# Splitting a weight chunk in four pieces ahead of the last squares, and splitting one chunk ahead in the second pass

## The chip, the core and the metric

The kernel runs on one core of a Trainium2 chip. The metric is the device time of one execution in microseconds. An execution is also profiled: the profile lists each instruction of TensorE (PE, and PEld for its weight loads), VectorE (DVE), ScalarE (ACT), GpSimd (POOL) and SyncE (SP, whose queue here issues most DMAs), with its start, its duration and what it waited for.

## The reference

One layer of a decoder trunk over 16 meta tokens and 256 tokens, of 2048 channels. What matters here is its beginning: the norm, and the combined projection whose columns are taken apart.

```python
h = jnp.concatenate([meta_b, x], axis=1)            # 16 + 256 rows of 2048
u = rms_norm(h, g_pre_mix[l])
proj = u @ w_in[l]
z_pool, v_conv, g_conv, gate_a, gate_b = jnp.split(proj, splits, axis=-1)
y_a = causal_multiscale_pool(z_pool, w_pool_grp[l], pool_scale[l]) @ w_pool_out[l]
y_b = conformer_conv(v_conv, g_conv, w_dw[l], b_dw[l],
                     conv_ln_g[l], conv_ln_b[l]) @ w_conv_out[l]
m = jax.nn.sigmoid(gate_a) * y_a + jax.nn.sigmoid(gate_b) * y_b
h = h + rms_norm(m @ w_o[l], g_post_mix[l])
u = rms_norm(h, g_pre_mlp[l])
f = jnp.square(jax.nn.relu(u @ w_up[l])) @ w_down[l]
h = h + rms_norm(f, g_post_mlp[l])
```

In `conformer_conv`, v times sigmoid(g) goes through a causal depthwise convolution of 31 taps. All is float32.

## The kernel before

**Weights come in chunks.** A chunk is 1 MB of float32: 128 partitions by 2048 columns. Its raw form is loaded by SyncE's queue into one of three rooms (`raws`, L252 and L254). It is then split in two numbers, a high part (a copy to fp32r on ScalarE, L259) and a low part (raw minus high on VectorE, L262), and PE multiplies with both: `mm3` (L447) issues three matmuls for each 128 x 128 block, high weights with u's high part, high weights with u's low part, low weights with u's high part. There are three rooms each for raw, high and low. So chunk n is loaded when the low part of chunk n-3 has been made, and its high part is written when PE is done with chunk n-3.

**The first pass** (chunks 0 to 3, `FIRST` = 4) makes the first 256 columns each of v and g for all 272 tokens, four accumulators wide, while x is still coming in. It is a loop over the 16 blocks of 128 channels: product k on PE (`product_of`), transposes of x for the blocks to come (`x_tile`: PE L396, then the scaled high and low parts of u at L397 and L398), and the splits of the weights' rows (`row`), of which each chunk has four here. Into the same loop are put the squares of x and of the meta tokens, halves of a row block at a time (`squares_of`, L406, on ScalarE, in place), whose sums give the norm. The meta tokens' natural layout, `m_in`, is loaded for these squares alone (L355); `x_in` is the layout of x's blocks.

After product 13 chunk 4 is split whole. After the loop `scale_roots` (L420 to L431) takes the roots and makes diagonals of them, `diag`; there a small activation (`warm_up`) brings in the table that holds the sigmoid.

**The second and third pass** are calls of `project`, for v and for g of the next 256 columns; each uses two chunks (4 and 5, then 6 and 7). Ahead of each chunk's matmuls `fetch` splits the chunk and those that follow, up to two ahead, and opens (loads) them where they are not open yet. After each half of the columns `drain` issues what is pending: after the first half of chunk 4 `after_first`, which turns the diagonals into a row of scales (`pb` on PE, L437; copied to `rb` on VectorE, L439) and applies it to the first pass's v (L520); after the second half `tap_columns`, which transposes rows of vectors (L326) and the taps (L589) on PE into PSUM tiles of the same two rooms that pb comes from, and g's part (L527). Later drains issue the convolution, tap by tap (L513 on VectorE).

Every engine works through its own list in the order in which the program issues it: the schedule is written out by hand. PE, ScalarE and VectorE meet only at data and at rooms that have to come free.

The chunks' loads are issued on SyncE's queue in this order: x block 0 and chunk 0 interleaved, x block 1, chunk 1, x block 2, chunk 2 in four loads, x block 3, `m_in`, chunk 3 in four loads, chunk 4, 5, 6 and so on.

Of the kernel before, what the change touches and what calls it, by code (L numbers as in the profile page):

```python
# [10 lines left out]
AF = mybir.ActivationFunctionType  # L11
# [5 lines left out]
CW = 512  # L17
# [83 lines left out]
def hybrid_block(ctx: ExitStack, tc: tile.TileContext, ins: dict, out: bass.AP):  # L101
    nc = tc.nc
    x = ins["x"][0]
    meta = ins["meta"]
    T, D = x.shape
    M = meta.shape[0]
    L = M + T
    NT = T // P
    KD = D // P
    w_in = ins["w_in"][0]  # L110
    w_grp = ins["w_pool_grp"][0]
    NG, GD, _ = w_grp.shape
# [22 lines left out]
    def f32(ap):  # L135
        return ap.bitcast(F32)
# [18 lines left out]
    def flush(n=0):  # L155
        while len(late) > n:
            late.pop(0)()
# [28 lines left out]
    HALF = (2 * CK, CW // 2)  # L186
# [4 lines left out]
    FIRST = len(stream)  # L191
# [35 lines left out]
    def part_tile(tag, n, standing=False):  # L227

        key = f"{tag}{n % 3}"
        room = ready.pop(key) if key in ready else part_room(key, f"{tag}_{n}")  # L230
        place = 2 if standing and tag == "hi" else 1
        shift = (place - 1 - 3 * KEYS.index(key)) % 4 * LINE
        return room[:, shift:shift + CK * CW]

    def open_chunk(loads=None):

        n = at["n"]
        at["n"] += 1
        src, (rows, width) = stream[n]
        raw = raws.tile([P, CK * CW], F32, tag="raw", name=f"raw_{n}")  # L240
        hi, lo = (part_tile(tag, at["parts"], n in standing_chunks) for tag in ("hi", "lo"))
        at["parts"] += 1
        flat, (raw, hi, lo) = raw, (t.rearrange("p (k c) -> p k c", k=rows) for t in (raw, hi, lo))
        if n < FIRST:
            dst = raw.rearrange("p k (h c) -> p k h c", h=2)
            for load in loads or [(slice(i, i + 2), BOTH, nc.sync) for i in range(0, rows, 2)]:
                if callable(load):
                    load()
                    continue
                sl, halves_, queue = load  # L250
                for k in range(sl.start, sl.stop):
                    queue.dma_start(dst[:, k, halves_], src[:, k, halves_])  # L252
        else:
            nc.sync.dma_start(raw, src)  # L254
        pieces = rows if n < FIRST else 1
        k = rows // pieces

        def high(sl, cs):
            nc.scalar.copy(hi[:, sl, cs], raw[:, sl, cs])  # L259

        def low(sl, cs):
            nc.vector.tensor_sub(lo[:, sl, cs], raw[:, sl, cs], f32(hi[:, sl, cs]))  # L262

        def piece(i, cs):
            def f():
                sl = slice(i * k, (i + 1) * k)
                high(sl, cs)
                low(sl, cs)
            return f
        todo = [piece(i, slice(0, width)) for i in range(pieces)]  # L270
        if n == 0:
            todo[:1] = [piece(0, slice(h * HALF_CW, (h + 1) * HALF_CW)) for h in range(2)]
        opened.append((hi, lo, todo, flat))

    def split_pieces(c):
        while opened[c][2]:
            opened[c][2].pop(0)()

    def fetch(ahead=2):

        for c in range(ahead + 1):
            if c == len(opened) and at["n"] < len(stream):
                open_chunk()
            if c < len(opened):
                split_pieces(c)
        flush()
        return opened.pop(0)[:2]
# [10 lines left out]
    def warm_up(func):  # L298

        nc.scalar.activation(warm, ones[:, 0:1], func)  # L300
# [3 lines left out]
    m_in = big.tile([M, D], F32, tag="a", name="m_in")  # L304
# [9 lines left out]
    def load_rows(queue, *names):  # L314
        rows = tmp.tile([48, P], F32, tag="g", name=f"rows_{names[0]}")
        n = 0
        for name in names:
            v = ins[name][0].rearrange("(k p) -> k p", p=P)
            queue.dma_start(rows[n:n + v.shape[0], :], v)
            n += v.shape[0]  # L320
        return rows, n, names[0]
# [10 lines left out]
    def load_x(queue, b, ts=slice(0, NT), cs=(0, 2)):  # L332

        sl = slice(b * CW + cs[0] * CW // 2, b * CW + cs[1] * CW // 2)
        queue.dma_start(x_in[:, ts, sl], xv[:, ts, sl])
# [14 lines left out]
    load_x(nc.sync, 1)  # L350
    open_chunk()
    load_x(nc.sync, 2)
    open_chunk()
    load_x(nc.sync, 3)
    nc.sync.dma_start(m_in, meta)  # L355
    other_rows = load_rows(nc.gpsimd, "pool_scale", "b_dw", "conv_ln_g", "conv_ln_b", "g_pre_mlp")
    taps_in = big.tile([TAPS, CC], F32, tag="c", name="taps_in")
    nc.gpsimd.dma_start(taps_in, w_dw)
# [13 lines left out]
    u = big.tile([P, KD, 2, -(-L // (4 * LINE)) * 4 * LINE], F32R, tag="um", name="u")[:, :, :, :L]  # L372
# [29 lines left out]
    def squares_of(t, b):  # L402

        sl = slice(b * D // 2, (b + 1) * D // 2)
        src, n = (x_in[:, t, sl], P) if t < NT else (m_in[:, sl], M)
        nc.scalar.activation(src, src, AF.Square, accum_out=ssq[:n, t, b:b + 1])  # L406

    def rsqrt(r, q, var):

        nc.vector.reciprocal(r, q)  # L410
        nc.vector.tensor_mul(q, r, r)
        nc.vector.tensor_mul(q, q, var)
        nc.vector.tensor_scalar(q, q, -0.5, 1.5, op0=ALU.mult, op1=ALU.add)
        nc.vector.tensor_mul(r, r, q)
# [3 lines left out]
    def scale_roots():  # L418
        tot = tmp.tile([P, NT + 1], F32, tag="tot", name="tot0")
        nc.vector.reduce_sum(tot, ssq, axis=mybir.AxisListType.X)  # L420
        nc.vector.tensor_scalar(tot, tot, 1.0 / D, RMS_EPS, op0=ALU.mult, op1=ALU.add)
        sc["r"] = r = const.tile([P, NT + 1], F32, name="r_in")
        q = tmp.tile([P, NT + 1], F32, tag="rs", bufs=1, name="rs_q_in")
        nc.scalar.activation(q, tot, AF.Sqrt)
        warm_up(AF.Sigmoid)
        rsqrt(r, q, tot)
        sc["diag"] = []
        for t in range(NT + 1):
            n = P if t < NT else M
            dg = tmp.tile([P, P], F32, tag="v", bufs=5, name=f"diag_{t}")  # L430
            nc.vector.tensor_scalar_mul(dg[:n, :n], ident[:n, :n], r[:n, t:t + 1])  # L431
            sc["diag"].append(dg)

    def scale_rows():
        pb = misc_tile("pb")
        for t, lo_, n in [(NT, 0, M)] + [(t, M + t * P, P) for t in range(NT)]:
            nc.tensor.matmul(pb[:, lo_:lo_ + n], ones[:n, :], sc["diag"][t][:n, :n],  # L437
                             start=True, stop=True)
        nc.vector.tensor_copy(rb, pb[:, :L])  # L439
# [27 lines left out]
    def acc_tiles(name, n=CW // P):  # L467
        return [acc_tile(f"acc_{name}_{j}") for j in range(n)]

    def project(act, nk, evac, name, mm=mm2, width=CW, shape=HALF, fill=0.0):  # L470

        ck, cw = shape
        accs = [acc[:, :width] for acc in acc_tiles(name, cw // P)]
        for kc in range(nk // ck):
            hi, lo = fetch()
            for j, acc in enumerate(accs):
                for k in range(ck):
                    kk = kc * ck + k
                    mm(acc, hi, lo, act, (k, kk), slice(j * P, (j + 1) * P), kk == 0, kk == nk - 1)
                if kc == nk // ck - 1:  # L480
                    flush(1)
                    evac(j, acc)
                if fill:
                    drain(fill * P / cw)
# [59 lines left out]
    def row(k):  # L544
        opened[k // CK][2].pop(0)()
# [13 lines left out]
    for k in range(KD):  # L559
        product_of(k)  # L560
        if k % CK == CK - 1:
            open_chunk()
        if k in (0, 2):
            for kx in (k + 2, k + 3):
                x_tile(kx)
                row(kx)
        elif k % 2 == 0 and k + 3 < KD:
            x_pair(k + 2)
        elif k + 3 < KD and k > 1:
            row(k + 3)  # L570
            row(k + 4)
        squares = {6: (0, 0), 8: (NT, 0), 10: (1, 0), 12: (NT, 1), 14: (0, 1), 15: (1, 1)}
        if k in squares:
            squares_of(*squares[k])
        if k == 13:
            split_pieces(FIRST)
    del opened[:FIRST]
    scale_roots()

    def after_first():  # L580
        scale_rows()
        for j, acc in enumerate(accs[:2]):
            evac_v(j, acc)
# [13 lines left out]
    pending += [(0, after_first), LATER, (0, tap_columns)]  # L597
    pending += [(0, lambda j=j: evac_g(0)(j, accs[2 + j])) for j in range(2)]
    for h in range(1, CC // HALF_CW):
        project(u, KD, evac_v, f"v{h}", mm=mm3, width=L, fill=2.5)  # L600
        project(u, KD, evac_g(h * HALF_CW // P), f"g{h}", mm=mm3, width=L, fill=2.4)


# [148 lines left out]
    hi, lo = fetch()  # L752
# [522 lines left out]
    hi, lo = fetch()  # L1275
# [80 lines left out]
    def load(r):  # L1356
        src, (rows, width) = source(*r)
        room = room_at[r] = free_rooms.pop(0)
        plan.add("SP", 3.2, lambda: nc.sync.dma_start(
            room_of[room].rearrange("p (k c) -> p k c", k=rows), src),  # L1360
            writes=(f"raw{room}",), late=2.0)
# [373 lines left out]
    for e, cs in enumerate(col_halves):  # L1735
        for w, s in ends:
            h = AT[s][0]
# [53 lines left out]
```

## Time and profile before

| | |
|---|---|
| runs shown | 1210.0 us median of 3 (1209.54 to 1210.31) |
| the profiled execution's own time | 1210.1 us |
| its span in the profile | 1208.3 us |
| PE busy | 1196.3 us, 99% |
| VectorE busy | 974.6 us, 81% |
| ScalarE busy | 625.4 us, 52% |
| mean granted TensorE clock | 0.996 |

The span runs from the first instruction to the last; the execution's own time is 1.8 us longer. In a row of the timeline stand the start, the duration, the engine, the line of the code, the operation, what is written from what, the shape, and how many instructions are merged in the row; in brackets is how long the engine was idle before it, and what ended that. In a list of waits stand who waited for whom, and the microseconds in total, the count and the longest. A row of the stretches gives the stretch, its length, the busy time of PE, PEld, VectorE, ScalarE and GpSimd with the number of instructions, the granted clock, the DMA engines' share and GB/s. A row on DMAs gives the destination and source, the queue, the count, the size and the time from the start of the issue to the landing.

### The profile page before, as it was taken

What the parts mean: (1) busy time and instruction counts of PE and PEld (TensorE: products, weight loads), DVE (VectorE), ACT (ScalarE), POOL (GpSimd) and SP (SyncE); (2) the same over time, 40 slices, a digit from 0 to 9 for tenths busy, and PEclk for the clock granted to TensorE, in tenths of its full rate; (3) what the DMA queues carried; (4) which work ended last, traced back from release to release, by engine and by line L of the source; (5) the groups of instructions that cost most, each with busy time, mean ns of one, the idle gap of its engine ahead of it and who ended that gap; (6) DMA issues with size and microseconds to landing.
All of it is one profiled execution on the core that took longest, in us unless ns stands there. A gap on an engine that the chain in (4) does not pass through costs nothing.

```text
span 1208.3 us, 15702 instructions
## 1 busy us (share of the span) xinstructions
PE 1196.3 (99%) x6444; PEld 1039.1 (86%) x6444; DVE 974.6 (81%) x1051; ACT 625.4 (52%) x630; POOL 8.3 (1%) x19
## 2 busy tenths in 40 slices
PE   9999999999999999999999999999999999999997
PEld 9899988888888888898888888888888888888886
DVE  5799988999766778678988878878788778788756
ACT  6533334444584455566555554564555555555543
POOL 1000000000000000000000000000000000000000
PEclk9999999999999999999999999999999999999999
DMA  9655556555648578546475574674764855755841
GB/s 292 202 182 176 175 176 206 182 203 183 201 142 281 177 253 266 201 139 222 150 259 174 170 236 159 202 242 144 241 209 146 268 192 161 244 174 170 276 147 69
DMA packets 162678, 238.40 MB, mean 197 GB/s; under 512 B 4161, under 2 KB 92417, under 8 KB 162080
## 3 DMA queue, kind: packets, MB, share of 16 engines
q1 hardware_dynamic: 160032, 230.77, 58.1%
q0 software_dynamic: 1680, 5.40, 1.7%
q8 instruction: 50, 0.82, 0.3%
q10 hardware_dynamic: 896, 1.25, 0.3%
q14 instruction: 20, 0.16, 0.0%
HBM read 235.30 MB, written 2.10 MB: 196 GB/s over the span
## 4 chain that ended last, share of the span: by engine, by line
PE 98%; DVE 1%; ACT 1%; issue 0%; DVEq 0%; ACTq 0%
PE bank_u L452 18%; PE acc_gate L712 14%; PE acc_up L1546 14%; PE bank_u L458 9%; PE bank_a L1546 7%; PE o_c L1050 6%; PE bank_b L1546 5%; PE acc_z L447 4%; PE acc_co L712 4%; PE acc_po L712 4%; PE acc_g L447 3%; PE acc_v L447 3%; PE acc_vg L447 2%; PE acc_up L452 1%; PE bank_u L1546 1%; PE o_a L1050 1%
## 5 line engine op out<-in xcount | busy, mean ns | idle before, releaser
L452 PE MATMUL bank_u<-m,hi 128*128 128x512 f32 x960 | 329.9, 390 | 0.0
L458 PE MATMUL bank_u<-m,lo 128*128 128x256 f32 x960 | 265.5, 277 | 0.0
L259 ACT CAST hi<-raw 128x2048 fp32r<-128x2048 f32 (+2 forms) x91 | 150.8, 1666 | 196.9 <-PE acc_gate L712 67.7
L1397 DVE TENSOR_TENSOR lo<-raw_m,hi 128x2048 fp32r<-128x2048 f32 x85 | 194.4, 2290 | 59.5 <-ACT hi L1392 59.3
L1392 ACT CAST hi<-raw_m 128x2048 fp32r<-128x2048 f32 x85 | 162.5, 1912 | 138.0 <-PE bank_u L452 74.5
L262 DVE TENSOR_TENSOR lo<-raw,hi 128x2048 fp32r<-128x2048 f32 (+2 forms) x91 | 179.9, 1984 | 47.5 <-ACT hi L259 47.0
L452 PEld LDWEIGHTS bank_u<-m,hi 128*128 128x128 f32 x960 | 180.2, 188 | 38.0
L458 PEld LDWEIGHTS bank_u<-m,lo 128*128 128x128 f32 x960 | 180.3, 188 | 1.6
L712 PE MATMUL acc_gate<-hi,u 128*128 128x512 f32 x512 | 158.4, 390 | 0.0
L1546 PE MATMUL acc_up<-hi,forms 128*128 128x512 f32 x496 | 157.5, 389 | 0.0
L513 DVE SCALAR_TENSOR_TENSOR c<-a,taps,c 128x256 f32<-128x256 f32 x240 | 115.6, 483 | 6.7
L712 PEld LDWEIGHTS acc_gate<-hi,u 128*128 128x128 f32 x512 | 96.1, 188 | 19.9
L1546 PEld LDWEIGHTS acc_up<-hi,forms 128*128 128x128 f32 x496 | 93.1, 188 | 19.5
L712 PE MATMUL acc_gate<-lo,u 128*128 128x512 f32 x256 | 99.6, 389 | 0.0
L1546 PE MATMUL acc_up<-lo,forms 128*128 128x512 f32 x248 | 96.6, 389 | 0.0
L1397 DVE TENSOR_TENSOR lo<-raw_c,hi 128x2048 fp32r<-128x2048 f32 x29 | 66.4, 2289 | 20.9 <-ACT hi L1392 20.9
L1546 PE MATMUL bank_a<-hi,forms 128*128 128x512 f32 (+1 forms) x256 | 82.0, 383 | 0.0
L1392 ACT CAST hi<-raw_c 128x2048 fp32r<-128x2048 f32 x29 | 55.3, 1907 | 50.9 <-PE bank_u L452 27.9
L1397 DVE TENSOR_TENSOR lo<-raw_a,hi 128x2048 fp32r<-128x2048 f32 x29 | 66.4, 2289 | 17.9 <-ACT hi L1392 17.9
L1392 ACT CAST hi<-raw_a 128x2048 fp32r<-128x2048 f32 x29 | 55.4, 1910 | 42.4 <-PE bank_u L452 19.4
L1050 PE MATMUL o_c<-hi,m 128*128 128x512 f32 x208 | 65.6, 390 | 0.0
L1546 PE MATMUL bank_b<-hi,forms 128*128 128x512 f32 (+1 forms) x200 | 63.7, 382 | 0.0
(317 smaller groups left out, 1856.4 us busy)
## 6 DMA issues: line engine op xcount, KB each, us to landing
raw<-in_w_in_dram SPq DMA_DIRECT2D x52, 1024.0 KB, 5.1
raw_m<-in_w_down_dram SPq DMA_DIRECT2D x37, 1024.0 KB, 5.3
raw_m<-in_w_up_dram SPq DMA_DIRECT2D x33, 1024.0 KB, 6.1
raw_c<-in_w_down_dram SPq DMA_DIRECT2D x14, 1024.0 KB, 5.2
raw_a<-in_w_up_dram SPq DMA_DIRECT2D x13, 1024.0 KB, 6.8
raw_a<-in_w_down_dram SPq DMA_DIRECT2D x13, 1024.0 KB, 5.3
raw_c<-in_w_up_dram SPq DMA_DIRECT2D x12, 1024.0 KB, 5.9
raw_o<-in_w_o_dram SPq DMA_DIRECT2D x10, 1024.0 KB, 7.2
```

Source lines behind the costliest of these rows:

```text
L259: nc.scalar.copy(hi[:, sl, cs], raw[:, sl, cs])
L262: nc.vector.tensor_sub(lo[:, sl, cs], raw[:, sl, cs], f32(hi[:, sl, cs]))
L447: nc.tensor.matmul(acc, w[:, k[0], cs], act[:, k[1], a, off:], start=first and n == 0, stop=last and n == 2)
L452: nc.tensor.matmul(acc.rearrange("p (a t) -> p a t", a=2)[:, :, ts], hi[:, k[0], cs], act[:, k[1], :, off + ts.start:off + ts.stop], start ...
L458: nc.tensor.matmul(acc[:, :T], lo[:, k[0], cs], act[:, k[1], 0, off:], start=False, stop=stop, skip_group_check=True)
L513: nc.vector.scalar_tensor_tensor(c, conv["a"][:, q, i:i + T], taps[:, q, i:i + 1], c, op0=ALU.mult, op1=ALU.add)
L712: nc.tensor.matmul(acc, act(kk)[:, a_, ts_], w_[:, k, :], start=kk == 0 and n == 0, stop=kk == nk - 1 and n == 2)
L1050: nc.tensor.matmul(acc, form(k, a_), box[w_][:, k, :], start=start and k == 0 and n == 0, stop=stop and k == CK - 1 and n == 2, skip_group ...
L1392: nc.scalar.copy(box["flat"], raw)
L1397: nc.vector.tensor_sub(lo, raw, f32(box["flat"]))
L1546: nc.tensor.matmul(acc, forms[h][:, f, k, a_, :], box[w_][:, k, cs], start=start and k == 0 and n == 0, stop=stop and k == KH - 1 and n == ...
```

## The change

The diff has five parts.

1. Chunk 4 (`n == FIRST`) is split in four pieces of 512 columns rather than whole. The first piece follows the rows 14 and 15 after product 11, the other three follow the loop.
2. The squares move: the first half of the meta tokens' goes to product 4, x's first halves to products 6 and 8, the meta tokens' second half to product 10, and x's second halves behind the loop, after the pieces.
3. The load of `m_in` goes on SyncE's queue from behind x block 3 to in front of chunk 2.
4. The call that brings in the sigmoid's table goes from `scale_roots` to the head of `after_first`.
5. `project` and `fetch` take the number of chunks to split ahead; in the second pass it is one. So chunk 6 is split ahead of chunk 5's matmuls, and chunk 7 is opened and split with chunk 8 at the start of the third pass.

```diff
-        pieces = rows if n < FIRST else 1
+        pieces = rows if n < FIRST else 4 if n == FIRST else 1
...
     load_x(nc.sync, 2)
+    nc.sync.dma_start(m_in, meta)
     open_chunk()
     load_x(nc.sync, 3)
-    nc.sync.dma_start(m_in, meta)
...
         nc.scalar.activation(q, tot, AF.Sqrt)
-        warm_up(AF.Sigmoid)
         rsqrt(r, q, tot)
...
-    def project(act, nk, evac, name, mm=mm2, width=CW, shape=HALF, fill=0.0):
+    def project(act, nk, evac, name, mm=mm2, width=CW, shape=HALF, fill=0.0, ahead=2):
...
-            hi, lo = fetch()
+            hi, lo = fetch(ahead)
...
-        squares = {6: (0, 0), 8: (NT, 0), 10: (1, 0), 12: (NT, 1), 14: (0, 1), 15: (1, 1)}
+        squares = {4: (NT, 0), 6: (0, 0), 8: (1, 0), 10: (NT, 1)}
         if k in squares:
             squares_of(*squares[k])
-        if k == 13:
-            split_pieces(FIRST)
+        if k == KD - 5:
+            row(KD)
+    for _ in range(3):
+        row(KD)
+    for t in range(NT):
+        squares_of(t, 1)
     del opened[:FIRST]
     scale_roots()
 
     def after_first():
+        warm_up(AF.Sigmoid)
         scale_rows()
...
-        project(u, KD, evac_v, f"v{h}", mm=mm3, width=L, fill=2.5)
+
+        project(u, KD, evac_v, f"v{h}", mm=mm3, width=L, fill=2.5, ahead=1 if h == 1 else 2)
```

## The prediction

> **What bounds the kernel now.** I read the page's totals first, then the list of who waited for whom on PE, then PE's timeline where those waits fall.
>
> ```profile
> span 1208.3 us, 15702 instructions
> PE 1196.3 (99%) x6444; PEld 1039.1 (86%) x6444; DVE 974.6 (81%) x1051; ACT 625.4 (52%) x630; POOL 8.3 (1%) x19
> ```
>
> ```profile
> PE taps_t L589 <- DVE rb L439: 1.6, 1, 1.6
> PE acc_v L447 <- DVE lo L262: 1.2, 1, 1.2
> PE idle L366 <- DVE rb L291: 1.1, 1, 1.1
> ```
>
> PE is the bound from start to end: it is busy for 99% of the span, and its waits on other engines number three, 3.9 us together. The last row is the start of the kernel, which the change does not touch. The other two lie between 34 and 45 us, just where the change works. So the change can gain little more than those two waits and what hangs on them, and it can lose wherever it makes PE wait anew. Here they are on PE's timeline (start, duration):
>
> ```profile
> 33.93 0.41 PE L447 MATMUL acc_v<-u,hi 128*128 128x272 f32 x2
> 35.51 0.39 PE L447 MATMUL acc_v<-u,lo 128*128 128x272 f32 x1 [1.17 <-DVE lo L262]
> 35.74 0.41 PE L447 MATMUL acc_v<-u,hi 128*128 128x272 f32 x2
> ...
> 38.42 1.03 PE L437 MATMUL pb<-diag,ones 16*128 16x16 f32 x6
> ...
> 42.36 0.26 PE L326 MATMUL pv_pool_scale<-ident,rows_pool_scale 48*128 48x48 f32 x1
> 44.20 0.68 PE L589 MATMUL taps_t<-ident,taps_in 31*128 31x31 f32 x8 [1.58 <-DVE rb L439]
> 44.81 0.52 PE L447 MATMUL acc_v<-u,hi 128*128 128x272 f32 x2
> ...
> 49.06 0.41 PE L447 MATMUL acc_v<-u,hi 128*128 128x272 f32 x2
> ...
> 52.40 0.41 PE L447 MATMUL acc_g<-u,hi 128*128 128x272 f32 x2
> ```
>
> The first pass ends at 33.93. The second pass runs its first two matmuls (high weights of chunk 4) and then waits for the low weights of that chunk. At 42.36 the transposes of the row vectors begin, and those of the taps wait 1.58 us, because their PSUM tile is the one that held pb, which VectorE has not yet copied to rb. A third loss is not a wait. The granted clock halves behind the second gap:
>
> ```profile
> 46.00:47.00 1.00, 1.00 (x7) 1.00 (x6) 1.00 (x2) 0.62 (x2) 0.00 (x0) 0.50 1.11 354
> ```
>
> Behind the five engines' busy times stands the granted clock: 0.50 in this microsecond, with 7 matmuls in it (at 0.124 each it would be 8). VectorE shows why both waits exist:
>
> ```profile
> 33.16 2.29 DVE L262 TENSOR_TENSOR lo<-raw,hi 128x2048 fp32r<-128x2048 f32 x1 [2.31 <-ACT hi L259]
> 35.37 0.15 DVE L420 TENSOR_REDUCE tot<-ssq 128x3 f32<-128x6 f32 x1
> ...
> 37.00 0.62 DVE L431 TENSOR_SCALAR diag<-ident,r_in 128x128 f32<-128x128 f32 x3
> 39.30 4.49 DVE L262 TENSOR_TENSOR lo<-raw,hi 128x2048 fp32r<-128x2048 f32 x2 [1.69 <-ACT hi L259]
> 43.72 0.43 DVE L439 COPY rb<-pb 128x272 f32<-128x272 f32 x1
> ```
>
> Chunk 4's low part ends at 35.45, 1.5 us after PE came for it. The copy to rb stands behind the low parts of chunks 5 and 6 (two of them in 4.49 us), although pb's matmuls, from 38.42, take about 1.0.
>
> **What the change takes from the path.** From 49.06 to 52.40 are 27 matmuls in 3.34 us, so 0.124 each at the full clock. The pair at 35.74 was due at 33.93 + 3 x 0.124 = 34.30: the first wait costs 1.44. The second costs its idle time, 1.58. Behind it the second half of the pass, 48 matmuls, takes 52.40 - 44.81 = 7.59 against 48 x 0.124 = 5.94: 1.65 for the halved clock, of which I count 0.1 as the refill that any break brings, so 1.55. Sum 4.6 us (4.7 if the refill is regained too).
>
> **Chunk 4 in pieces.** The rows of ScalarE for it, in order, with what stands ahead of them:
>
> ```profile
> 15.83 0.84 ACT L397 ACTIVATE u<-xt,vecs 128x256 fp32r<-128x256 f32 x2 [0.63 <-PE xt L396]
> 17.89 1.22 ACT L259 CAST hi<-raw 128x512 fp32r<-128x512 f32 x2 [1.22 <-DMA raw<-in_w_in_dram]
> ...
> 27.82 1.13 ACT L259 CAST hi<-raw 128x512 fp32r<-128x512 f32 x2
> 29.47 0.84 ACT L397 ACTIVATE u<-xt,vecs 128x256 fp32r<-128x256 f32 x2 [0.51 <-PE xt L396]
> ...
> 31.24 1.89 ACT L259 CAST hi<-raw 128x2048 fp32r<-128x2048 f32 x1
> 33.03 1.05 ACT L406 ACTIVATE x_in<-x_in 128x1024 f32<-128x1024 f32 x1
> ...
> 35.03 0.18 ACT L406 ACTIVATION_READ_ACCUMULATOR x_in<-x_in 128x1 f32 x1
> 35.76 0.20 ACT L424 ACTIVATE rs_q_in<-tot 128x3 f32<-128x3 f32 x1 [0.55 <-DVE tot L421]
> 35.98 1.28 ACT L300 ACT_TABLE_LOAD   x1
> ...
> 37.39 3.70 ACT L259 CAST hi<-raw 128x2048 fp32r<-128x2048 f32 x2
> ```
>
> ```profile
> 28.47 1.29 DVE L262 TENSOR_TENSOR lo<-raw,hi 128x512 fp32r<-128x512 f32 x2 [1.03 <-ACT hi L259]
> 29.98 0.88 DVE L398 SCALAR_TENSOR_TENSOR u<-xt,vecs,u 128x256 fp32r<-128x256 f32 x2 [0.21 <-ACT u L397]
> ```
>
> A piece has 2 x 256 columns, the size of one row of the first chunks: two casts take 1.13, two lows 1.29. Four pieces are then at most 2.26 against 1.89 on ScalarE and 2.58 against 2.29 on VectorE. Both have idle time to take the 0.3 to 0.4. The first piece comes behind the casts at 27.82 and runs from 28.95 to about 29.5, in the 0.51 us in which ScalarE waited for PE's transposes. The activations of columns 14 and 15 stay at 29.5. The other three start at 30.3 and end by 32.0, since the square of the tokens that stood there has moved ahead. VectorE: lows of rows 14 and 15 until 29.76, the first piece's low until 30.4, the two u lows until 31.25 (the first by 30.85), three pieces until 33.2. PE wants chunk 4 at 33.93, so this wait goes with 0.7 to spare. The tight place is u's low of column 14: done at 30.85, and PE's product 14, two products of 12 matmuls ahead of 33.93, wants it with its second matmul, near 31.1. The bounds here are 0 and, if chunk 4 lands late, what its lateness exceeds 0.2 by.
>
> ```profile
> 20.74 0.41 PE L447 MATMUL acc_vg<-u,hi 128*128 128x272 f32 x2
> ...
> 19.50 0.37 SPq L254 DMA_DIRECT2D raw<-in_w_in_dram  x1
> raw<-in_w_in_dram SPq DMA_DIRECT2D x1, 1024.0 KB, 9.3
> 13.80 0.35 SPq L355 DMA_DIRECT2D m_in<-in_meta_dram  x1
> 10.00:20.00 10.00, 10.00 (x82) 9.88 (x81) 7.17 (x14) 6.35 (x15) 0.00 (x0) 1.00 1.08 343
> ```
>
> Chunk 4 lands at 19.50 + 9.3 = 28.8, and its first piece can start at 28.95: just in time. The bytes ahead of it on SyncE's queue are the same as before, so I take no delay.
>
> **The meta load and the squares.** The load of m_in goes from 13.80 to in front of chunk 2's four loads and x's last block. At the 343 GB/s of the last row its 128 KB shift these by 0.38. Row 8 of the weights, for which ScalarE waited until 17.89 (its row among those of ScalarE says so), then comes at 18.3, and m_in, ahead of it in the queue, by then at the latest. Its square, taken as long as the others (1.05), follows the activations at 15.83 (0.84) and ends at 17.7, or at 19.3 if m_in comes last. In the first case rows 8 and 9 are cast from 18.3 to 19.5, VectorE's two lows end near 20.2 and u's low of column 8 half of 0.88 later, at 20.65. PE's product 8 begins with the pair at 20.74 and wants it for the second of them, at 20.86: nothing lost, with 0.2 to spare. In the second all this is 0.9 to 1.0 later, and about 0.7 is lost. I take 0.1. The other squares only change places, and ScalarE's later waits for PE take up the shift. The last two squares end with the three pieces plus their own 35.21 - 33.03 = 2.18: at 34.1, 1.1 earlier than before, so diag ends at 36.5 in place of 37.62. PE needs it after 24 matmuls from 33.93, at 36.9: covered by 0.4; without this cover each late microsecond is one of PE.
>
> **The sigmoid table and the second pass.** The load of the table leaves the place ahead of chunk 5's cast. That cast starts near 34.85 instead of 37.39, its low runs 36.75 to 39.05, and the copy to rb, with no chunk 6 ahead of it, ends at 39.5. On PE pb takes at most 1.0, so the second column half ends by 36.9 + 1.0 + 3.0 = 40.9, and the taps' transposes find their tile free: the second wait goes with over 1 us to spare. The table load, 1.41 with its call until 37.39, now lies between the casts of chunks 5 and 6: chunk 6's high part ends at 40.1, and its low, behind rb, v, the taps' copy and g, at about 45.1. PE wants it at 47.5.
>
> Chunk 7 is split only at the start of the third pass, together with chunk 8, behind the last v and three taps:
>
> ```profile
> 52.60 0.44 DVE L520 TENSOR_TENSOR v<-acc_v,rb 128x272 f32<-128x272 f32 x1 [1.08 <-PE acc_v L447]
> 52.96 1.51 DVE L513 SCALAR_TENSOR_TENSOR c<-a,taps,c 128x256 f32<-128x256 f32 x3
> 54.47 2.29 DVE L262 TENSOR_TENSOR lo<-raw,hi 128x2048 fp32r<-128x2048 f32 x1
> ```
>
> From PE's end of the second pass at 47.5 that is 1.95 for v and taps and 2.29 for the low: 51.8, wanted at 47.5 + 5.94 = 53.4. It is covered by 1.6, the thinnest cover behind the first pass. Chunk 8's low ends at 54.1, wanted at 59.4. Opening chunk 7 later holds no load back: its room frees when chunk 4's low ends (33.2), chunk 8's at 39.05, and with the 9.3 of chunk 4, the slowest here, they are in at 42.5 and 48.4, ahead of their lows at 49.5 and 51.8.
>
> **The sum.** 4.6 gained, 0.1 lost: 4.5. The profiled execution was 1210.1, its span 1208.3; the runs have their median at 1210.0. 1210.1 - 4.5 = 1205.6. Nothing behind 52.4 shows a wait of PE, so it reaches the end.
>
> [...] The halved clock follows a gap of 1.58 us. [...]
>
> **Rivals.** *The clock still falls once.* [...] The changed kernel has small matmuls there too (pb, pv, taps). Against: the one stretch of the run at 0.50 stands behind the longest gap. 1205.6 + 1.55 = 1207.2. *A new small wait.* m_in last (0.7), chunk 4 later by a microsecond (0.8), or chunk 7's low behind its cover: 1206.3 to 1207.5. *The gain is given back.* The waits move to chunk 7 because VectorE is full there; its low would have to be later by 1.6 + 4 us: 1209.6. Against: the rows from 52.60 have 1.08 idle. *Slower.* One mechanism: m_in, a load onto 16 partitions, holds up SyncE's queue ahead of chunk 2, and rows 8 to 15 and then chunk 4 come late by D. ScalarE works in order, so PE loses about D - 0.2. It breaks even at D = 4.8, and at D = 8 the time is 1213. Against: in its old place the load had a slot among the others and nothing behind it came late.
>
> **How the numbers follow.** Forecast 0.64; clock 0.12; small wait 0.13; given back 0.06; slower 0.05. The forecast's own range is 1205.2 to 1206.3. For 8 in 10 I go up to the clock's case and the worst small wait, and down by the run-to-run 0.4 and the refill: 1204.7 to 1207.6. A measurement tells 0.2% (2.4 us) from nothing, that is 1207.6: faster takes the forecast, two thirds of the clock's case and most of the small waits, 0.81; same 0.14; slower 0.05.
>
> **What would show it.** PE's wait list keeps only the start's row; chunk 4's low appears as four of 0.69 ending near 33.2; rb's copy starts near 39; the second pass ends near 47.5 to 48; no stretch at 0.50. I am wrong if PE waits in products 8 to 14, if it waits for the low of chunk 7 near 53, or if the clock falls without a gap.

## The result, and the profile after

The changed kernel's median is 1206.66 us over 13 executions (1206.50 to 1208.38), that of the kernel before, beside it, 1210.00 over 13 (1208.99 to 1211.56). The ratio is 0.9974 with a 95% interval of 0.9966 to 0.9983. The forecast was 1205.6, with a range of 1204.7 to 1207.6: the direction and the range held, and a median gain of 3.3 us stands where 4.4 was forecast. The time lies outside the narrower range that the prediction gave its own forecast (1205.2 to 1206.3), and inside that of its rival of a new small wait (1206.3 to 1207.5). The profiled execution took 1206.63 us, its span 1204.5 (before: 1210.1 and 1208.3).

PE's list of waits after the change. The two waits of before are gone, and a small one is new, in product 8; a wait of PE in products 8 to 14 was one of the prediction's own signs of being wrong:

```profile
PE idle L366 <- DVE rb L291: 1.1, 1, 1.1
PE acc_vg L446 <- DVE u L398: 0.2, 1, 0.2
```

PE's timeline at the places that the prediction showed (the lines of the code have moved by one to four):

```profile
7.06 0.37 PE L446 MATMUL acc_vg<-u,hi 128*128 128x272 f32 x1
...
21.14 0.28 PE L446 MATMUL acc_vg<-u,hi 128*128 128x272 f32 x1
21.63 0.39 PE L446 MATMUL acc_vg<-u,hi 128*128 128x272 f32 x1 [0.20 <-DVE u L398]
...
34.81 0.41 PE L446 MATMUL acc_v<-u,hi 128*128 128x272 f32 x2
...
37.86 1.03 PE L436 MATMUL pb<-diag,ones 16*128 16x16 f32 x6
...
41.79 0.26 PE L326 MATMUL pv_pool_scale<-ident,rows_pool_scale 48*128 48x48 f32 x1
41.98 0.68 PE L593 MATMUL taps_t<-ident,taps_in 31*128 31x31 f32 x8
42.59 0.52 PE L446 MATMUL acc_v<-u,hi 128*128 128x272 f32 x2
...
48.63 0.41 PE L446 MATMUL acc_g<-u,hi 128*128 128x272 f32 x2
```

The second pass, from the first acc_v to the first acc_g, takes 48.63 - 34.81 = 13.82, against 52.40 - 33.93 = 18.47 before: 4.65 less. But the pass ahead of it ends 0.88 later, at 34.81. So the span falls by 3.8, and the 0.88 is to be explained. The clock's row for the microsecond that was at 0.50 before:

```profile
46.00:47.00 1.00, 1.00 (x10) 1.00 (x9) 1.00 (x4) 0.47 (x1) 0.00 (x0) 1.00 0.00 0
```

It is at 1.00 now. VectorE, whose results both waits were for:

```profile
31.94 1.89 DVE L262 TENSOR_TENSOR lo<-raw,hi 128x512 fp32r<-128x512 f32 x3
35.31 0.16 DVE L420 TENSOR_REDUCE tot<-ssq 128x3 f32<-128x6 f32 x1 [1.49 <-ACT x_in L406]
...
36.95 0.62 DVE L430 TENSOR_SCALAR diag<-ident,r_in 128x128 f32<-128x128 f32 x3
37.74 2.29 DVE L262 TENSOR_TENSOR lo<-raw,hi 128x2048 fp32r<-128x2048 f32 x1 [0.18 <-ACT hi L259]
39.95 0.43 DVE L438 COPY rb<-pb 128x272 f32<-128x272 f32 x1
```

Chunk 4's last three pieces end at 33.83, a microsecond ahead of PE. The copy to rb follows chunk 5's low part alone and ends at 40.4, 1.6 ahead of the taps at 41.98. ScalarE, in the first pass, shows what is new:

```profile
17.42 1.06 ACT L406 ACTIVATE m_in<-m_in 16x1024 f32<-16x1024 f32 x1 [0.35 <-DMA m_in<-in_meta_dram]
18.38 0.18 ACT L406 ACTIVATION_READ_ACCUMULATOR m_in<-m_in 16x1 f32 x1
18.47 0.60 ACT L259 CAST hi<-raw 128x512 fp32r<-128x512 f32 x1
19.83 0.62 ACT L259 CAST hi<-raw 128x512 fp32r<-128x512 f32 x1 [0.76 <-DMA raw<-in_w_in_dram]
```

It waits 0.35 for m_in, and then 0.76 for row 9 of the weights, which is in at 19.83. Before, rows 8 and 9 were cast together from 17.89.

### The profile page after: what moved, and what is told of

It is laid out like the page before. It is cut to its first block, busy times and chain, and to the rows that moved or that the text cites. A ratio compares the mean times of both kernels' runs of the same rounds, so it can differ in the third digit from the quotient of the medians.

```text
span 1204.5 us, 15705 instructions
## 1 busy us (share of the span) xinstructions
PE 1195.1 (99%) x6444; PEld 1038.0 (86%) x6444; DVE 974.3 (81%) x1054; ACT 625.2 (52%) x633; POOL 8.3 (1%) x19
## 4 chain that ended last, share of the span: by engine, by line
PE 97%; DMA 2%; DVE 1%; ACT 0%; ACTq 0%; DVEq 0%; issue 0%
PE bank_u L451 18%; PE acc_gate L717 14%; PE acc_up L1551 14%; PE bank_u L457 9%; PE bank_a L1551 7%; PE o_c L1055 6%; PE bank_b L1551 5%; PE acc_z L446 4%; PE acc_co L717 4%; PE acc_po L717 4%; PE acc_v L446 3%; PE acc_g L446 3%; PE acc_up L451 1%; PE acc_vg L446 1%; PE bank_u L1551 1%; DMA x_in<-in_x_dram 1%
```

## The experiments

Eleven runs were made in three groups, each timed against the kernel before on the same chip. From each one's profile I take when the first product starts, which varies from one execution to the next (see the end), the length of the first pass (first product to the second pass), that of the second pass, and how much of the second pass lies ahead of the taps' transposes. An instant of one profile can be compared with that of another only from such a common event.

| kernel | median us | before beside it | first product | first pass | second pass | to the taps | gap ahead of the taps |
|---|---|---|---|---|---|---|---|
| before | 1210.00 | | 6.67 | 27.26 | 18.47 | 10.27 | 1.58 |
| the change | 1206.66 | 1210.00 | 7.06 | 27.75 | 13.82 | 7.17 | none |
| first_pass_only | 1210.51 | 1210.26 | 7.58 | 27.25 | 19.04 | 9.35 | 2.11 |
| second_pass_only | 1207.49 | 1210.26 | 7.09 | 27.35 | 15.26 | 8.61 | none |
| two_ahead | 1207.51 | 1210.26 | 6.93 | 27.61 | 14.49 | 7.85 | 0.59 |
| m_in_other_queue | 1207.32 | 1210.26 | 6.50 | 28.93 | 13.82 | 7.18 | none |
| m_in_back | 1206.48 | 1210.45 | 7.36 | 27.31 | 13.82 | 7.17 | none |
| table_back | 1206.67 | 1210.45 | 6.45 | 28.04 | 13.82 | 7.18 | none |
| whole_chunk | 1206.92 | 1210.45 | 7.47 | 27.19 | 14.22 | 7.58 | none |
| gap_5 | 1211.47 | 1210.45 | 7.51 | 27.73 | 16.47 | 9.82 | 2.58 |
| changed_again | 1206.65 | 1209.51 | 7.17 | 27.85 | 13.82 | 7.18 | none |
| m_in_back_again | 1206.48 | 1209.51 | 7.45 | 27.17 | 13.82 | 7.18 | none |
| gap_3 | 1207.72 | 1209.51 | 6.71 | 27.97 | 15.01 | 8.37 | 1.12 |

### One half of the change at a time

`first_pass_only` keeps the pieces, the squares and the meta load, and undoes the rest:

```diff
     def after_first():
-        warm_up(AF.Sigmoid)
...
         nc.scalar.activation(q, tot, AF.Sqrt)
+        warm_up(AF.Sigmoid)
...
-        project(u, KD, evac_v, f"v{h}", mm=mm3, width=L, fill=2.5, ahead=1 if h == 1 else 2)
+        project(u, KD, evac_v, f"v{h}", mm=mm3, width=L, fill=2.5)
```

> Parts 1 to 3 alone (pieces, squares, meta load); the table load and two chunks ahead as before. Theory: the copy to rb again stands behind the low parts of chunks 5 and 6, and their chain starts from the last square, which ends at the same moment in both profiles (diag done at 37.6 in both). So the taps' transposes start near 44.2 as before: the first wait goes, the second grows from 1.6 to about 2.2 us, the clock falls as before, and the time is that of before, 1209.5 to 1210.5. Rival (the terms of the sum are independent): the second wait stays at 1.6 and the time falls by the first wait less what product 8 loses, to about 1209.0.

PE and VectorE in its profile:

```profile
34.83 0.41 PE L447 MATMUL acc_v<-u,hi 128*128 128x272 f32 x2
...
44.18 0.98 PE L593 MATMUL taps_t<-ident,taps_in 31*128 31x31 f32 x8 [2.11 <-DVE rb L439]
...
39.28 4.49 DVE L262 TENSOR_TENSOR lo<-raw,hi 128x2048 fp32r<-128x2048 f32 x2 [1.68 <-ACT hi L259]
43.69 0.43 DVE L439 COPY rb<-pb 128x272 f32<-128x272 f32 x1
```

The wait for chunk 4's low is gone. The taps start at 44.18, almost the 44.20 of before, but that is a coincidence: in this profile the first product came 0.91 later, and the second pass began at 34.83 rather than 33.93. Counted from the start of the second pass the taps come after 9.35 us, against 10.27 before. So 0.92 of the first wait's 1.44 is gained, and 0.53 of it goes into the gap, which grows from 1.58 to 2.11. The copy to rb came forward with the squares: the last square ended 1.28 behind the start of the second pass before (35.21 against 33.93), and ends with it here (34.84).

Yet the median is that of before (ratio 1.0003, interval 0.9994 to 1.0013). Behind the taps the pass takes 9.69 in this profile, against 8.20, because the clock is at half for about twice as long (3.41 us in the profile of before; here its mean from 44 to 52 is 0.57, which makes about 6.9); and by their times 9 of the 11 executions have a halved clock, against 19 of 33 before (see the section on the clock). The two others, 1208.49 and 1208.77, are 0.4 to 0.7 below the lower group of before. The time and the gap came as the theory said, but not for its reason: it compared moments of two profiles that began differently. The rival does not hold either, since the gap grew. The two waits are partly coupled, and what the first gave did not show in the median.

`second_pass_only` is the kernel before with parts 4 and 5:

```diff
     def after_first():
+        warm_up(AF.Sigmoid)
...
         nc.scalar.activation(q, tot, AF.Sqrt)
-        warm_up(AF.Sigmoid)
...
-        project(u, KD, evac_v, f"v{h}", mm=mm3, width=L, fill=2.5)
+        project(u, KD, evac_v, f"v{h}", mm=mm3, width=L, fill=2.5, ahead=1 if h == 1 else 2)
```

> Parts 4 and 5 alone (table load moved, one chunk ahead); chunk 4 split whole after product 13, squares and meta load as before. Theory: the first wait stays at 1.2 us; the copy to rb follows chunk 5's low part alone and ends near 40.5, ahead of PE's arrival at 42.4, so the second wait and the halved clock go: 1.58 + 1.55 less, about 1206.9. Rival (the clock falls for another reason than the second wait, or after the first one alone): one stretch at half clock stays, about 1208.5.

```profile
36.01 0.39 PE L446 MATMUL acc_v<-u,lo 128*128 128x272 f32 x1 [1.17 <-DVE lo L262]
...
42.86 0.26 PE L326 MATMUL pv_pool_scale<-ident,rows_pool_scale 48*128 48x48 f32 x1
43.05 0.61 PE L589 MATMUL taps_t<-ident,taps_in 31*128 31x31 f32 x7
```

The first wait stays at 1.17, the taps follow the vectors at once, and the clock stays up: behind the start of the taps the pass takes 6.65, as in the change, against 8.20 before. The median is 1207.49 against 1210.26, 2.8 less where 3.1 was expected: most of the change's gain. The second pass is 18.47 - 15.26 = 3.21 shorter; with the whole change it is 4.65 shorter, so the pieces and squares add 1.44, the price that the prediction put on the first wait.

### What removed the second wait: one chunk ahead, or the table load

`two_ahead` undoes part 5 alone, and leaves the table load where the change put it:

```diff
-        project(u, KD, evac_v, f"v{h}", mm=mm3, width=L, fill=2.5, ahead=1 if h == 1 else 2)
+        project(u, KD, evac_v, f"v{h}", mm=mm3, width=L, fill=2.5)
```

> The changed kernel with two chunks split ahead in the second pass again; the table load stays moved. Theory: chunk 6's low part stands ahead of the copy to rb, but both casts start 1.4 us earlier than before for want of the table load; rb ends near 42.6 and the taps' transposes, ready at 42.0, wait about 0.7 us: 1207.4 if the clock holds, 1209.0 if it falls. Rival (one chunk ahead is not what matters): no wait at the taps, 1206.7.

```profile
37.49 4.49 DVE L262 TENSOR_TENSOR lo<-raw,hi 128x2048 fp32r<-128x2048 f32 x2 [0.18 <-ACT hi L259]
41.90 0.43 DVE L438 COPY rb<-pb 128x272 f32<-128x272 f32 x1
```

PE waits 0.59 at the taps, and the median is 1207.51, in line with the theory's 1207.4. `table_back` undoes only part 4, by the same four lines as in first_pass_only.

> The changed kernel with the sigmoid's table load back ahead of chunk 5's cast. Theory: chunk 5's cast and low part and with them the copy to rb come 1.4 us later, rb ends near 41.8, just at the time when PE is ready for the taps (42.0): no wait or at most 0.3 us, time within 0.3 of the changed kernel. Rival (the moved table load is what removed the second wait): a wait of about 1 us at the taps and the halved clock in some runs, 1207.7 or more.

```profile
38.96 2.29 DVE L262 TENSOR_TENSOR lo<-raw,hi 128x2048 fp32r<-128x2048 f32 x1 [1.69 <-ACT hi L259]
41.17 0.43 DVE L439 COPY rb<-pb 128x272 f32<-128x272 f32 x1
```

The copy to rb ends at 41.60, 0.07 ahead of the taps (41.67 there), and PE does not wait: 1206.67, the changed kernel's time. So one chunk ahead suffices without the table load. But the table load is not worth nothing: first_pass_only and two_ahead differ by its place alone, and there it brings the gap from 2.11 to 0.59 and the median from 1210.51 to 1207.51. Counted from the start of the second pass, the copy to rb ends after 9.29 us in first_pass_only, 7.79 in two_ahead, 7.11 in table_back and 5.57 in the changed kernel. So moving the table load brings it 1.5 forward, and splitting one chunk ahead 2.2, where the gap of 2.11 has to go. Each alone takes most or all of the wait, so their gains do not add: behind the one the other has next to nothing left to gain.

### Pieces, or place

`whole_chunk` splits chunk 4 whole, at the place of the last three pieces:

```diff
-        pieces = rows if n < FIRST else 4 if n == FIRST else 1
+        pieces = rows if n < FIRST else 1
...
-        if k == KD - 5:
-            row(KD)
-    for _ in range(3):
-        row(KD)
+    row(KD)
```

> The changed kernel with chunk 4 split whole behind the loop rather than in four pieces. Theory: the cast runs 31.1 to 33.0, the low part to 35.3, PE wants it at 35.1: a wait of 0.2 to 0.5 us, time 0.2 to 0.5 more than the changed kernel; most of the first wait is removed by the place ahead of the squares, little by the pieces. Rival (the pieces are what matters): the wait of 1.2 us is back, 1207.9.

```profile
34.66 0.41 PE L446 MATMUL acc_v<-u,hi 128*128 128x272 f32 x2
35.20 0.39 PE L446 MATMUL acc_v<-u,lo 128*128 128x272 f32 x1
...
32.86 2.29 DVE L262 TENSOR_TENSOR lo<-raw,hi 128x2048 fp32r<-128x2048 f32 x1 [1.28 <-ACT hi L259]
```

The low part ends at 35.15, and the third matmul starts 0.54 after the pair rather than 0.25. The second pass is 0.40 longer (14.22), and the median 0.26 above the changed kernel's. So of the 1.44, the place ahead of the squares brings 1.0 and the pieces 0.4, by one profile of each. The medians differ by less, and their ranges overlap; the execution outside the span is 0.3 longer with the pieces (see the rest of the difference, below).

### Why the first pass got longer

`m_in_other_queue` takes the load of m_in off SyncE's queue:

```diff
-    nc.sync.dma_start(m_in, meta)
     open_chunk()
     load_x(nc.sync, 3)
...
     nc.gpsimd.dma_start(taps_in, w_dw)
+    nc.gpsimd.dma_start(m_in, meta)
```

> The changed kernel with the load of m_in issued on GpSimd's queue behind the taps' load. Theory: row 9 of the weights was late because SyncE issues a load only when the eighth load before it has landed, and m_in took a slot in front of chunk 2; without it row 9 is issued near 9.7 in place of 11.4, lands near 18.5 in place of 19.8, and PE has no wait in product 8: 0.4 to 0.5 less than the changed kernel, about 1206.2. Rival (the 128 KB alone delay it, whichever queue carries them): row 9 still lands near 19.8 and the wait in product 8 stays, about 1206.7.

```profile
PE xt L396 <- DMA x_in<-in_x_dram: 1.5, 1, 1.5
```

The wait in product 8 went, but a wait of 1.5 us came at 13.4, for x's second block. On GpSimd's queue the load of m_in ran from 4.69 to 13.02, beside that block, which came in at 13.22 where it came in at 11.41 in the changed kernel. That the one made the other late is the likely reading, from one profile. The first pass is the longest of all. The expectation failed. Row 9 was issued at 9.61, as the theory has it, but came in at 19.74, as the rival has it, and since everything behind 13.4 is shifted, the run does not decide between them. It does show that the 0.38 reckoned from the bytes need not be the whole price of such a load.

`m_in_back` leaves the load where it was before the change and orders the squares accordingly:

```diff
-    nc.sync.dma_start(m_in, meta)
     open_chunk()
     load_x(nc.sync, 3)
+    nc.sync.dma_start(m_in, meta)
...
-        squares = {4: (NT, 0), 6: (0, 0), 8: (1, 0), 10: (NT, 1)}
+        squares = {4: (0, 0), 6: (1, 0), 8: (NT, 0), 10: (NT, 1)}
```

> The changed kernel with the load of m_in back behind x's last block, and the squares in the order x first halves (products 4 and 6), meta tokens (8 and 10). Theory: the wait in product 8 came from m_in's slot ahead of chunk 2 (row 9 issued 1.7 us later and landed 1.4 us later); with the old order row 9 lands near 18.4, PE has no wait in product 8, and the time falls by 0.4 to 0.5 against the changed kernel. Rival (row 9 comes late for another reason, such as ScalarE's new square at product 4): a wait of 0.2 to 0.5 in product 8 stays and the time is the changed kernel's.

It has no wait in product 8, and its first pass takes 27.31. As its first product started late (7.36), I ran it once more, with the changed kernel beside it.

> The kernel with the load of m_in back behind x's last block, a second time. Theory: no wait in product 8, the first pass takes 27.3, and the median is 0.3 to 0.5 below that of the changed kernel beside it. Rival (its first profile was an accident of a late start): a wait in product 8, no difference of the medians.

> The changed kernel as it is, for a comparison on one chip with the next one. Theory (m_in's slot ahead of chunk 2 makes row 9 late): ScalarE waits again for row 9 of the weights, and the first pass, from its first product to the second pass, takes 27.5 to 28.0 us against 27.3 before the change; PE's wait in product 8 is 0.2 to 0.5. Rival: the wait of the first profile was an accident, and the pass takes 27.3.

ScalarE in the profile of m_in_back_again, and the issue of row 9 there, with the time to landing:

```profile
17.23 1.06 ACT L406 ACTIVATE x_in<-x_in 128x1024 f32<-128x1024 f32 x1
18.18 0.20 ACT L406 ACTIVATION_READ_ACCUMULATOR x_in<-x_in 128x1 f32 x1
18.27 1.14 ACT L259 CAST hi<-raw 128x512 fp32r<-128x512 f32 x2
...
10.20 0.37 SPq L252 DMA_DIRECT2D raw<-in_w_in_dram  x1
raw<-in_w_in_dram SPq DMA_DIRECT2D x1, 256.0 KB, 7.2
```

Here ScalarE has a square at product 4 as well, and rows 8 and 9 follow it without a wait; row 9 was issued at 10.20 and in at 17.4. In the changed kernel:

```profile
11.43 0.37 SPq L252 DMA_DIRECT2D raw<-in_w_in_dram  x1
raw<-in_w_in_dram SPq DMA_DIRECT2D x1, 256.0 KB, 8.4
```

Issued at 11.43, in at 19.83. In the profile of before it was issued at 9.76 and in 8.7 later, at 18.46:

```profile
9.76 0.54 SPq L252 DMA_DIRECT2D raw<-in_w_in_dram  x1
raw<-in_w_in_dram SPq DMA_DIRECT2D x1, 256.0 KB, 8.7
```

So row 9 is late by its slot: it is issued 1.7 later and in 1.4 later, where 0.38 were the bytes. changed_again shows a wait of 0.35 in product 8 and a first pass of 27.85.

The slot is not all of it. In the eight profiles with m_in ahead of chunk 2 on SyncE's queue ScalarE waits for m_in itself in seven, 0.35 to 1.19 us, and m_in's square stands ahead of rows 8 and 9 in its list. In gap_5 it waits 1.19 for m_in and then for neither row, and PE still waits 0.3 in product 8. Of these eight six have a first pass of 27.6 to 28.0, and two (first_pass_only, whole_chunk) 27.2; both of m_in_back are at 27.2 and 27.3. But the two short ones began late (7.58 and 7.47), when PE comes later for the same loads, and so did both of m_in_back (7.36 and 7.45). So the profiles do not show what m_in_back gains in executions that begin early. In the medians the gain of m_in_back is 0.17 (1206.48 against 1206.65, ranges that overlap): it was expected at 0.3 to 0.5, and the times do not resolve it. Against the kernel before, m_in_back has ratios of 0.9967 (0.9954 to 0.9979) and 0.9973 (0.9963 to 0.9983).

### The clock and the gap

To see whether a gap brings the clock down, I put a gap back in. `gap_5` (`gap_3` with three) has work of no use on VectorE ahead of the copy to rb:

```diff
+        delay = tmp.tile([P, CW], F32, tag="junk", bufs=1, name="delay")
+        nc.vector.memset(delay, 0.0)
+        for _ in range(5):
+            nc.vector.tensor_add(delay, delay, delay)
         nc.vector.tensor_copy(rb, pb[:, :L])
```

> The changed kernel with work of no use on VectorE (a fill and five additions of 128x512) ahead of the copy to rb, which puts back a gap of about 1.9 us on PE ahead of the taps. [...]

> The changed kernel with a fill and three additions of 128x512 on VectorE ahead of the copy to rb: a gap of about 1.2 us ahead of the taps. [...]

```profile
45.06 0.68 PE L597 MATMUL taps_t<-ident,taps_in 31*128 31x31 f32 x8 [2.58 <-DVE rb L442]
43.05 0.68 PE L597 MATMUL taps_t<-ident,taps_in 31*128 31x31 f32 x8 [1.12 <-DVE rb L442]
```

The gaps are 2.58 and 1.12 (the additions took 0.72 each, more than I had reckoned). Neither profiled execution has the half clock behind its gap (the mean clock is 0.999 in both, and the rows from 45 to 46 and from 47 to 48 of gap_5 are at 1.00). The other executions tell by their times and, less sharply, by the mean granted clock that each of them lists:

| kernel | gap | executions near the time that the gap alone gives | executions above | their mean clock |
|---|---|---|---|---|
| two_ahead | 0.59 | 11 (1206.97 to 1208.37) | 0 | |
| gap_3 | 1.12 | 8 (1207.20 to 1208.11) | 3 (1209.07 to 1212.53) | 0.996 |
| second_pass_only | 1.17, at the first wait | 11 (1206.87 to 1208.13) | 0 | |
| before, first group | 1.58 | 14 (1208.97 to 1209.60) | 19 (1210.12 to 1213.80) | 0.996 or 0.997 |
| before, beside gap_5 | 1.58 | 3 (1209.33 to 1209.46) | 14 (1210.23 to 1211.63) | 0.996 or 0.997 |
| before, beside gap_3 | 1.58 | 14 (1208.96 to 1209.94) | 7 (1210.19 to 1210.90) | 0.996 or 0.997 |
| first_pass_only | 2.11 | 2 (1208.49, 1208.77) | 9 (1209.77 to 1212.57) | 0.995 to 0.997 |
| gap_5 | 2.58 | 3 (1208.90 to 1209.78) | 8 (1210.78 to 1212.90) | 0.995 or 0.996 |

Those near the gap's own time have mean clocks of 0.997 to 0.999 (one 0.996). The two overlap at 0.997, so the sorting goes by time, and a few times (1212.53 of gap_3, three from 1213.36 to 1213.80 of before) lie too far above for one fall of the clock. The times of gap_5 split in two, though not sharply; of gap_3's, 3 of 11 lie apart from the others. The executions above are none at 0.59, and some at every gap of 1.12 or more ahead of the taps. How their share grows with the length is not shown: the same kernel before has 7 of 21 on one chip and 14 of 17 on another, and beside it gap_3 and gap_5 have no more (3 of 11 and 8 of 11). The profiles of before and first_pass_only have the half clock behind gaps of 1.58 and 2.11.

In the profile of before the clock is first at full speed from 4.45 us on, at half from 45.41 to 48.82, which is 3.41 us, and at half once more from 1202.53 to the end (in that of the change only at the end, from 1200.35). The stretch from 45.41 on begins 1.21 behind the gap that ends at 44.20. The length of a gap alone does not decide: the gaps of 1.58 and 2.11 have the half clock behind them, those of 1.12 (gap_3), 1.17 (the first wait of before and of second_pass_only), 1.5 (m_in_other_queue, mean clock 0.999) and 2.58 (gap_5) do not. What else counts is not shown. In the profile of first_pass_only the clock is at half for about 6.9 us; two of its rows:

```profile
45.00:46.00 1.00, 1.00 (x6) 0.94 (x6) 0.87 (x4) 0.01 (x1) 0.00 (x0) 0.50 1.07 374
50.00:51.00 1.00, 1.00 (x6) 1.00 (x6) 0.07 (x1) 0.00 (x0) 0.00 (x0) 0.50 0.94 302
```

## Why the prediction was right, and where its sizes were off

**The two waits** went as forecast, and the sum of 4.6 is met in the profile: the second pass is 4.65 shorter. But its terms are not independent, as the prediction took them to be. The whole of the first wait's 1.44 is to be had only because the second wait goes too; alone it gave 0.92 in the profile of first_pass_only and nothing in the median. And the second wait had two remedies in the change, of which one chunk ahead is enough (table_back) and the table load alone leaves 0.59 (two_ahead).

**The halved clock** (1.55 in the sum) was taken from one profiled execution. That execution has it, but by their times 14 of the 33 executions of the first group do not. (The prediction read 7 matmuls in a microsecond against 8; in the same view the rows at full clock count 10 or 11, so the drop is larger than it says. The 0.1 that I took off for a refill behind a break is shown by no run: these 48 matmuls take 6.04 in the changed kernel, which has no gap there (48.63 - 42.59), and 6.03 behind the gap of gap_3 (49.69 - 43.66).) The two groups' middles are about 1209.2 and 1210.5, so where it comes it costs about 1.3. Against executions without it the change gains 1209.2 - 1206.66 = 2.5. Two waits (1.44 + 1.58) less product 8's 0.5 and less the 0.3 outside the span, below, would be 2.2; the 0.3 that is left is less than the start of the kernel varies. That the median of before lay in the group with the half clock is luck: most of the third term shows in the medians for that reason. In the third group, where it lay in the other, the changed kernel gains 2.9 (1209.51 against 1206.65). The gap gone, 12 of 13 executions of the changed kernel lie within 0.8 us.

**The step that failed** is the meta load: "its 128 KB shift these by 0.38 ... I take 0.1". It cost PE 0.47 in the profile: product 8 to the end took 21.14 to 23.45, 2.31, against 1.84 before (20.74 to 22.58, with the transposes). The prediction had two cases, m_in in time (nothing lost) and m_in last (0.7 lost), and took the first. The profile lies between: ScalarE waits 0.35 for m_in, whose square ends at 18.5 where the cases had 17.7 and 19.3, and then row 9 is late, which neither case has. For that row I had counted bytes and not slots. On SyncE's queue each of these loads is issued when the eighth before it has landed (in the trace it waits for the semaphore that the eighth load before it used, so this is how this program counts its loads; the six issued from 8.66 to 13.69 in the changed kernel follow that landing by 0.02 each): before, row 10 went at 11.54, as x's second block (issued at 4.75, 6.8 to landing) came in; with m_in in the row, row 9 stood at that place and went at 11.43. So m_in, only 128 KB, moved row 9 by a whole slot, 1.67 us. The prediction named this queue as the place of its slower rival, but there for a load that is slow in itself.

**The rest of the difference** has two parts. The first product started at 7.06 instead of 6.67 (0.39), which is the spread of the start and no part of the change. And the execution is 2.1 longer than its span and not 1.8, which the prediction did not have. This is no accident of one execution: in all 71 of before beside the experiments, in second_pass_only and in whole_chunk it is 1.7 to 1.9, and in the changed kernel and all other runs with chunk 4 in pieces 2.1 to 2.2, except gap_3 (1.85 to 2.14). So about 0.3 seems to come with the pieces, outside the span; by what is open. With the span's 4.65 - 0.49 - 0.39 = 3.8 this gives 1210.1 - 3.8 + 0.3 = 1206.6.

**The covers** held. Chunk 4 landed in time, PE did not wait for diag (it was ready 0.3 ahead of pb, where 0.4 was forecast; both came about a microsecond later than forecast, with the first pass), and chunk 7's low part was ready as reckoned, with 1.7 to spare where 1.6 was forecast:

```profile
48.83 0.44 DVE L519 TENSOR_TENSOR v<-acc_v,rb 128x272 f32<-128x272 f32 x1
49.18 1.52 DVE L512 SCALAR_TENSOR_TENSOR c<-a,taps,c 128x256 f32<-128x256 f32 x3
50.62 4.49 DVE L262 TENSOR_TENSOR lo<-raw,hi 128x2048 fp32r<-128x2048 f32 x2
```

The first of the two lows ends near 52.9, and PE wants it at 48.63 + 5.94 = 54.57.

## What to carry to other kernels

When an engine that works in order makes the bound engine wait twice in a row, look what the end of the second wait hangs on: as far as it does not come forward, removing the first wait alone only lengthens the second. When two moves each shorten the same wait, try each alone; their gains do not add. Work prefetched two steps ahead belongs behind any short operation on which the bound engine waits. A load moved forward in a queue can cost the loads behind it more than its bytes: m_in's were reckoned at 0.38 us, and row 9 was issued 1.67 later. And compare two profiles from a common event: equal times since the start can be a coincidence.

## What the runs showed of the hardware

Gaps of 1.58 and 2.11 us on PE were followed by a clock at half for 3.41 and about 6.9 us, in the profiles of before and first_pass_only; gaps of 1.12, 1.17 and 2.58 in those of gap_3, second_pass_only and gap_5 were not. By the times of the other executions this comes in a part of them, at gaps from 1.12 to 2.58 us ahead of the taps, and it makes the times of the kernel before fall in two groups 1.3 us apart.

The start of the kernel has a spread of its own. The same four transposes took 0.77 in the profile of before and 0.98 in that of the change:

```profile
4.80 0.77 PE L396 MATMUL xt<-ident,x_in 128*128 128x128 f32 x4
4.98 0.98 PE L396 MATMUL xt<-ident,x_in 128*128 128x128 f32 x4
```

Over the profiles the first product starts between 6.45 and 7.58, with the same instructions of PE ahead of it. The trace's record of the clock says full speed from 4.45 us in the profile of before, where it starts at 6.67, and from 5.69 in that of the change, where it starts at 7.06. The twelve small matmuls just ahead of it take 1.50 us in both, but 1.80 in m_in_back_again, where it starts at 7.45, and 1.93 in first_pass_only, where it starts at 7.58. A profile's early microseconds are therefore compared from the first product on.
